# Gate/up weights of a hybrid decoder layer: the low parts of half of the weights by an accumulating DMA, and four Winograd pairs instead of two in seven blocks

## The chip, the core and the metric

One core of a Trainium2 chip runs the whole layer in one launch. The metric is the device time of that launch in microseconds (us), taken by the chip. The kernel before was timed three times: 1114.35, 1113.87 and 1112.45 us, median 1113.87 us. A fourth execution was profiled; its own time is 1112.63 us, and the span from its first to its last instruction is 1110.9 us.

## What is computed

One decoder layer on 256 tokens of width 2048, in fp32. A combined projection feeds a gated linear recurrence and a chunked retention, their outputs go through an output projection into the residual stream, and a SwiGLU feed-forward block follows. The change touches the feed-forward block only:

```
u  = rmsnorm(h, ln2_w)
ff = silu(u @ w_ffn_gate) * (u @ w_ffn_up)      # 256 x 2048 @ 2048 x 5632, twice
h  = h + ff @ w_ffn_down                        # 256 x 5632 @ 5632 x 2048
out = rmsnorm(h, final_norm_w)
```

The result must have fp32 accuracy, while TensorE is fed with a shorter format (fp32r). So each operand is cut into a high part, which is the operand cast to fp32r, and a low part, operand minus high part, and a product is made of three matmuls: high times high, high times low, low times high.

## The kernel before

**Blocks, pairs, halves.** Gate and up weights are walked in 11 blocks of 512 columns (`ffn_block`, block 0 to 10). A block has 8 steps, and a step takes 256 rows of the weights. Such a piece is called a pair here (class `Quad`): four weight tiles of 128 x 512, b11 and b12 (gate and up of the first 128 rows), then b22 and b21 (up and gate of the second 128 rows). It is loaded as two halves of 128 x 1024, 512 KB each, into tiles `raw`. The two token halves of u make the left operands a11, a12, a21, a22 (class `Left`, 128 x 128 each, made once and used by all 11 blocks).

**Eight products or seven.** An ordinary pair takes the eight products of the list `EIGHT`: each of the four results c11, c21, c12, c22 gets two. A *summed* pair (steps in `SUMMED`) follows Winograd's form of Strassen's scheme and takes seven products (list `SEVEN`) from sums t1 to t4 of the weights and s1 to s4 of the left operands. The results are gathered in PSUM over all 8 steps: four banks c11 to c22 (pool `aux`, 4 banks) and, for summed pairs, p1, p5, p6, p7 (pool `bank`, 4 banks). A product is three matmuls with 512 columns (L658, L659, L660).

**Who does what.** SyncE (SP) issues the loads of `raw` (L605). ScalarE (ACT) casts: tile `wh` (128 x 1024) is the high part (L101). VectorE (DVE) subtracts: tile `wl` is the low part (L102). In a summed pair DVE also makes t1 to t4 (L619, L620, L622, L623) into two more tiles of the pool of `raw` (named `sum`), which are cut like weights; b11 alone goes to `bh` and `bl` (128 x 512). GpSimd (POOL) does nothing in this stage. After the last step `ffn_post` adds results (L720, L722), applies the gate (L696 to L698), and `turn` transposes them on TensorE (L705) into `ff`.

**Buffers.** `raw` and `sum` share 5 buffers, `wh` has 4, `wl` has 4, and everything of 128 x 512 (pool `acts`) 58. A load of `raw` can go out only when the buffer it gets has been read for the last time; a cast into `wh` only when PE has used that buffer for the last time.

**Order.** Each engine works through its own queue strictly in order, and waits at the head of the queue. The order in the queues is not the order of the code: a scheduler orders instructions when the kernel is built, by priority and by what it holds to be ready. So PE's queue of one step mixes products of neighbouring steps: matmuls that need only a high part come first.

Of the kernel before, what the change touches and what calls it, by code (L numbers as in the profile page):

```python
# [14 lines left out]
P = 128  # L15
# [13 lines left out]

SUMMED = (2, 4)
SUMMED_DOWN = (2, 6, 10, 14, 18)


# [1 line left out]
def tile_hymba_layer(ctx: ExitStack, tc: tile.TileContext, A: dict, out: bass.AP):  # L37
# [181 lines left out]
    def defer(steps, f):  # L219
        later.append([steps, f])  # L220
# [321 lines left out]
    def out_post(f, ps):  # L542
        x = xs(f)
        if f < KT - 2:
            t = act_tile("op")[:, :S]
            halves(ps, t)
            v.tensor_tensor(out=x, in0=x, in1=t, op=ALU.add)
        else:
            v.tensor_tensor(out=x, in0=ps[:, :S], in1=x, op=ALU.add)
        if f % 2 == 0:  # L550
            hf[0] = act_tile("hf")
        act.activation(out=hf[0][:, (f % 2) * S : (f % 2) * S + S], in_=x, func=AF.Copy, scale=col(C_LN2 + f))
        if f % 2:
            hh[f // 2] = Left(hf[0], f // 2 in SUMMED)
        sq = sumsq[:, :S] if f == 0 else act_tile("sq")[:, :S]
        act.activation(out=sq, in_=x, func=AF.Square)
        if f:
            v.tensor_tensor(out=sumsq[:, :S], in0=sumsq[:, :S], in1=sq, op=ALU.add)
# [30 lines left out]
    class Quad:  # L589

        def __init__(self, src, sums, before=None):
            self.src, self.sums, self.before = src, sums, before
            self.parts = {}

        def cut(self, names, raw):
            h, l = (wpool.tile([P, 1024], F32R, tag=g, name=nm(g)) for g in ("wh", "wl"))
# [4 lines left out]
        def load(self, half):  # L603
            r = rpool.tile([P, 1024], F32, tag="raw", name=nm("raw"))
            nc.sync.dma_start(out=r, in_=self.src[:, half * 1024 : half * 1024 + 1024])  # L605
            if half == 0 and self.before:
                self.before()
            if not self.sums:
                self.cut(("b22", "b21") if half else ("b11", "b12"), r)
                return  # L610
            if half == 0:
                self.ra = r
                self.parts["b11"] = act_tile("bh", F32R), act_tile("bl", F32R)
                split(*self.parts["b11"], r[:, :512])
                return
            b11, b12, b22, b21 = self.ra[:, :512], self.ra[:, 512:], r[:, :512], r[:, 512:]
            ta, tb = (rpool.tile([P, 1024], F32, tag="raw", name=nm("sum")) for _ in range(2))
            t1, t2, t3, t4 = ta[:, :512], ta[:, 512:], tb[:, :512], tb[:, 512:]
            v.tensor_tensor(out=t1, in0=b11, in1=b12, op=ALU.add)  # L619
            v.tensor_tensor(out=t2, in0=t1, in1=b22, op=ALU.add)  # L620
            self.cut(("t1", "t2"), ta)
            v.tensor_tensor(out=t3, in0=b12, in1=b22, op=ALU.add)  # L622
            v.tensor_tensor(out=t4, in0=t2, in1=b21, op=ALU.add)  # L623
            self.cut(("t3", "t4"), tb)
            self.cut(("b22", "b21"), r)

    EIGHT = (
        ("c11", "a11", "b11"), ("c11", "a12", "b21"), ("c21", "a21", "b11"), ("c21", "a22", "b21"),
        ("c12", "a11", "b12"), ("c12", "a12", "b22"), ("c22", "a21", "b12"), ("c22", "a22", "b22"),
    )  # L630
    SEVEN = (
        ("p1", "a11", "b11"), ("p5", "s1", "t1"), ("p6", "s2", "t2"), ("p7", "s3", "t3"),
# [40 lines left out]

    def ffn_block(j):
        def after(i):
            if j == 0 and i == SUMMED[-1] + 1:
                norm2()
            if j in (1, 2) and i < 2:
                resid_tok(2 * j - 2 + i)
            if j == NB - 1 and i == 0:  # L680
                load_fw()

        ps = {}
        quads = [Quad(A["w_gu"][j * (KT // 2) + i], i in SUMMED) for i in range(KT // 2)]
        block(quads, hh, ffn_post(j, ps), ps, after=after)

    def ffn_post(j, ps):
# [21 lines left out]
        def post(c):  # L709
            if c == "p1":  # L710
                part["c11"] = act_tile("c11")
                act.copy(out=part["c11"], in_=ps[c])
            elif c == "p7":
                n = act_tile("n")
                v.tensor_tensor(out=n, in0=ps["p6"], in1=part["c11"], op=ALU.subtract)
                other("c12", "c12", n, ps["p5"])
                other("c21", "c21", n, ps["p7"])
                other("c22", "c22", part["c21"], ps["p5"])
            elif c in ("c11", "c12", "c22"):
                v.tensor_tensor(out=part[c], in0=ps[c], in1=part[c], op=ALU.add)  # L720
            elif c == "c21":
                v.tensor_tensor(out=part[c], in0=ps[c], in1=part[c], op=ALU.subtract)  # L722
            if c == "c12":
                gated(0)
            if c == "c22":
                gated(1)
                defer(2, lambda: turn(0))
                defer(3, lambda: turn(1))

        return post  # L730

# [316 lines left out]
```

## Time and profile before

| | |
|---|---|
| three runs | 1112.45 to 1114.35 us, median 1113.87 us |
| profiled execution | 1112.63 us, span 1110.9 us, 1.73 us outside the span |
| granted TensorE clock | 0.996 |
| gate/up blocks | from about 392 to about 868 us, 43.1 us each in the middle |
| down projection | from there to about 1096 us |

In the profile, "busy" is the time in which an engine executes; a wait is idle time that ended when another engine or a transfer released it. Lines of the profile name an instruction by its source line, its engine and its tiles (out<-in). PE is TensorE, PEld its weight load.

### The profile page before, as it was taken

The page shows a single profiled execution, that of the slowest core. Times are in us where ns is not written, and L with a number is a line of the kernel's source. Part 1 is how long each engine was busy: PE and PEld are TensorE (multiplying, and loading weights), DVE is VectorE, ACT ScalarE, POOL GpSimd, SP SyncE. Part 2 cuts the span into 40 slices and gives each one's busy share as a digit, 9 for nine tenths or more (in the row PEclk, how much of TensorE's full clock was granted, in tenths as well). Part 3 has the DMA queues.
Part 4 walks back from the last instruction along what each step waited for, and adds up shares of the span by engine and source line. Part 5 has one row for each costly group of instructions (what it writes and reads, how often), then busy time and mean ns, then how long its engine had stood idle before and what let it go on. Part 6 is the DMA issues. An engine that isn't in the chain of part 4 may idle for free.

```text
span 1110.9 us, 15099 instructions
## 1 busy us (share of the span) xinstructions
PE 1096.1 (99%) x5584; PEld 934.2 (84%) x5584; DVE 878.0 (79%) x1229; ACT 617.3 (56%) x826; POOL 58.1 (5%) x64
## 2 busy tenths in 40 slices
PE   9999999999999999999999999999999999999995
PEld 7998888889988988888888888888888888888884
DVE  7797799978766787788778877877887988886665
ACT  7666644468465665554554555545546665554453
POOL 0602230000000000000000000000000000020001
PEclk9999999999999999999999999999999999999998
DMA  9764575554665555645746646656556456655662
GB/s 329 236 198 151 174 252 167 169 188 146 201 198 187 171 192 183 212 147 186 239 138 219 226 152 227 193 186 228 170 187 229 171 176 198 233 186 193 192 220 80
DMA packets 62218, 214.74 MB, mean 193 GB/s; under 512 B 7105, under 2 KB 7489, under 8 KB 62145
## 3 DMA queue, kind: packets, MB, share of 16 engines
q1 hardware_dynamic: 61344, 211.70, 57.8%
q0 software_dynamic: 512, 1.57, 0.4%
q8 instruction: 43, 0.70, 0.3%
q10 hardware_dynamic: 288, 0.52, 0.1%
q14 instruction: 31, 0.25, 0.1%
HBM read 211.67 MB, written 2.10 MB: 192 GB/s over the span
## 4 chain that ended last, share of the span: by engine, by line
PE 97%; ACT 1%; POOL 1%; DVE 0%; DMA 0%; issue 0%; SPq 0%; DVEq 0%; POOLq 0%
PE c L658 18%; PE c L659 18%; PE c L660 18%; PE fm L140 10%; PE fm L141 5%; PE fm L146 3%; PE fm L147 3%; PE fm L145 3%; PE p L660 3%; PE p L658 3%; PE p L659 3%; PE tm L156 3%; PE tm L157 3%; PE tm L158 3%; PE ft L705 1%; POOL sumsq L289 1%
## 5 line engine op out<-in xcount | busy, mean ns | idle before, releaser
L102 DVE TENSOR_TENSOR wl<-raw,wh 128x1024 fp32r<-128x1024 f32 (+1 forms) x368 | 440.7, 1209 | 151.2 <-ACT wh L101 149.4
L101 ACT CAST wh<-raw 128x1024 fp32r<-128x1024 f32 (+1 forms) x368 | 375.8, 1032 | 297.3 <-PE c L660 145.1
L659 PE MATMUL c<-wl,ah 128*128 128x512 f32 x864 | 333.1, 391 | 0.0
L660 PE MATMUL c<-wh,al 128*128 128x512 f32 x864 | 331.8, 389 | 0.0
L658 PE MATMUL c<-wh,ah 128*128 128x512 f32 x864 | 292.1, 389 | 0.0
L659 PEld LDWEIGHTS c<-wl,ah 128*128 128x128 f32 x864 | 162.2, 188 | 33.5 <-DVE wl L102 0.4
L658 PEld LDWEIGHTS c<-wh,ah 128*128 128x128 f32 x864 | 162.1, 188 | 33.4
L660 PEld LDWEIGHTS c<-wh,al 128*128 128x128 f32 x864 | 162.3, 188 | 33.0
L101 ACT CAST wh<-sum 128x1024 fp32r<-128x1024 f32 x64 | 66.8, 1054 | 81.3 <-PE c L660 52.7
L140 PE MATMUL fm<-u,wh 128*128 128x512 f32 x256 | 90.7, 398 | 0.0
L140 PE MATMUL fm<-y,wh 128*128 128x512 f32 x224 | 78.9, 398 | 0.0
L102 DVE TENSOR_TENSOR wl<-sum,wh 128x1024 fp32r<-128x1024 f32 x64 | 76.7, 1217 | 2.2 <-ACT wh L101 1.6
L146 PE MATMUL fm<-u,wh 128*128 128x256 f32 x256 | 72.7, 284 | 0.0
L145 PE MATMUL fm<-u,wh 128*128 128x256 f32 x256 | 72.7, 284 | 0.0
L147 PE MATMUL fm<-u,wl 128*128 128x256 f32 x256 | 72.3, 283 | 0.0
L141 PE MATMUL fm<-u,wl 128*128 128x256 f32 x256 | 71.9, 281 | 0.0
L141 PE MATMUL fm<-y,wl 128*128 128x256 f32 x224 | 62.4, 281 | 0.0
L807 POOL TENSOR_TENSOR htok<-htok,fw 128x512 f32<-128x512 f32 (+1 forms) x7 | 10.5, 1509 | 914.0 <-ACT junk L805 914.0
L140 PEld LDWEIGHTS fm<-u,wh 128*128 128x128 f32 x256 | 48.1, 188 | 11.7
L619 DVE TENSOR_TENSOR sum<-raw 128x512 f32<-128x512 f32 x32 | 22.0, 687 | 37.9 <-DMA raw<-in_w_down 23.0
L140 PEld LDWEIGHTS fm<-y,wh 128*128 128x128 f32 x224 | 41.9, 188 | 10.2
L146 PEld LDWEIGHTS fm<-u,wh 128*128 128x128 f32 x256 | 49.1, 192 | 0.1
(242 smaller groups left out, 1489.5 us busy)
## 6 DMA issues: line engine op xcount, KB each, us to landing
raw<-in_w_gu SPq DMA_DIRECT2D x176, 512.0 KB, 5.0
raw<-in_w_down SPq DMA_DIRECT2D x88, 512.0 KB, 5.1
raw<-in_w_out SPq DMA_DIRECT2D x32, 512.0 KB, 4.2
raw<-in_w_lx SPq DMA_DIRECT2D x16, 512.0 KB, 4.9
raw<-in_w_k SPq DMA_DIRECT2D x16, 512.0 KB, 3.7
raw<-in_w_q SPq DMA_DIRECT2D x16, 512.0 KB, 4.2
raw<-in_w_rg SPq DMA_DIRECT2D x16, 512.0 KB, 3.7
raw<-in_w_lg SPq DMA_DIRECT2D x16, 512.0 KB, 3.8
```

What stands on the lines that cost most here:

```text
L101: act.copy(out=dst_h, in_=src)
L102: v.tensor_tensor(out=dst_l, in0=src, in1=dst_h.bitcast(F32), op=ALU.subtract)
L140: pe.matmul(ps, wh, hl, start=first, stop=False)
L141: pe.matmul(ps[:, :S], wl, hl[:, :S], start=False, stop=last)
L145: pe.matmul(ps, wh, hl[:, :S], start=first, stop=False)
L146: pe.matmul(ps, wh, hl[:, S:], start=False, stop=False)
L147: pe.matmul(ps, wl, hl[:, :S], start=False, stop=last)
L156: pe.matmul(ps, ah, wh, start=first, stop=False)
L157: pe.matmul(ps, ah, wl, start=False, stop=False)
L658: pe.matmul(p, ah, bh, start=firsts[c] == m, stop=False)
L659: pe.matmul(p, ah, bl, start=False, stop=False)
L660: pe.matmul(p, al, bh, start=False, stop=last)
```

## The change

Seven blocks (`N_ADDED`, block 0 to 6) treat the second half of each pair (b22, b21) in a new way, `cut_added`: ACT casts the high part as before; ACT then writes minus the high part into two tiles `ln` of 128 x 512 (from the pool `acts`); and GpSimd issues for each of them a DMA of 256 KB, from SBUF to SBUF, that adds the raw weights to what stands there. The result is the low part that DVE's subtraction made before. That is 16 such DMAs a block, 112 in all.

In these blocks four pairs are summed (steps 1, 3, 4, 6) in place of two (2, 4); blocks 7 to 10 keep 2 and 4. Left operands are summed for the five steps of both lists. A summed pair cuts its second half before its sums, not after. `EIGHT` is in another order, for all blocks: the four products with b11 and b12 come first. `norm2` runs after step 6 of block 0 (after step 5 before), and both transposing steps of `turn` run after the first step of the next block (the second one a step later before).

```
-SUMMED = (2, 4)
+SUMMED = (1, 3, 4, 6)
+SUMMED_LATE = (2, 4)
+N_ADDED = 7
...
-            hh[f // 2] = Left(hf[0], f // 2 in SUMMED)
+            hh[f // 2] = Left(hf[0], f // 2 in SUMMED + SUMMED_LATE)
...
+        def cut_added(self, names, raw):
+            h = wpool.tile([P, 1024], F32R, tag="wh", name=nm("wh"))
+            act.copy(out=h, in_=raw)
+            for n, name in enumerate(names):
+                hn, l = h[:, n * 512 : n * 512 + 512], act_tile("ln", F32R)
+                act.activation(out=l, in_=hn.bitcast(F32), func=AF.Copy, scale=-1.0)
+                pool.dma_start(out=l.bitcast(F32), in_=raw[:, n * 512 : n * 512 + 512], accum_op=ALU.add)
+                self.parts[name] = hn, l
...
-                self.cut(("b22", "b21") if half else ("b11", "b12"), r)
+                (self.cut_added if half and self.added else self.cut)(("b22", "b21") if half else ("b11", "b12"), r)
...
             v.tensor_tensor(out=t2, in0=t1, in1=b22, op=ALU.add)
+            (self.cut_added if self.added else self.cut)(("b22", "b21"), r)
             self.cut(("t1", "t2"), ta)
...
             self.cut(("t3", "t4"), tb)
-            self.cut(("b22", "b21"), r)
...
-        ("c11", "a11", "b11"), ("c11", "a12", "b21"), ("c21", "a21", "b11"), ("c21", "a22", "b21"),
+        ("c11", "a11", "b11"), ("c21", "a21", "b11"), ("c12", "a11", "b12"), ("c22", "a21", "b12"),
...
-            if j == 0 and i == SUMMED[-1] + 1:
+            if j == 0 and i == SUMMED[-1]:
                 norm2()
...
-        quads = [Quad(A["w_gu"][j * (KT // 2) + i], i in SUMMED) for i in range(KT // 2)]
+        added = j < N_ADDED
+        sums = SUMMED if added else SUMMED_LATE
+        quads = [Quad(A["w_gu"][j * (KT // 2) + i], i in sums, added=added) for i in range(KT // 2)]
...
-                defer(3, lambda: turn(1))
+                defer(2, lambda: turn(1))
```

The scheduler orders the queues anew. Two places matter for the prediction. In the rows below a number behind a name only tells tiles apart, and line numbers of the changed kernel are larger than those of the profile.

**Place 1, the border between two blocks.** PE's queue before, up to the first matmul into the next block's c11 (here c11_1204; the block that ends has c12_1127 and c22_1128):

```order
L658 MATMUL c12_1127_5849<-wh_1185_6095,ah_785_4339 128x512
L659 MATMUL c12_1127_5849<-wl_1186_6096,ah_785_4339 128x512
L660 MATMUL c12_1127_5849<-wh_1185_6095,al_786_4340 128x512
L658 MATMUL c22_1128_5856<-wh_1182_6065,ah_785_4339 128x512
L659 MATMUL c22_1128_5856<-wl_1183_6066,ah_785_4339 128x512
L660 MATMUL c22_1128_5856<-wh_1182_6065,al_786_4340 128x512
L658 MATMUL c22_1128_5856<-wh_1185_6095,ah_785_4339 128x512
L659 MATMUL c22_1128_5856<-wl_1186_6096,ah_785_4339 128x512
L660 MATMUL c22_1128_5856<-wh_1185_6095,al_786_4340 128x512
L658 MATMUL c11_1204_6189<-wh_1188_6101,ah_634_3518 128x512
```

The new c11 gets the bank of the old c11, whose last matmul stands 17 rows ahead of it. PE's queue now, at the border between blocks 4 and 5 (old results c11_1222, c12_1224, c22_1225, new c11_1321), from the last matmul that uses wh_1277:

```order
L673 MATMUL c11_1222_6100<-wh_1277_6331,al_773_4221 128x512
L671 MATMUL c11_1222_6100<-wh_1285_6351,ah_795_4370 128x512
L672 MATMUL c11_1222_6100<-wl_1286_6352,ah_795_4370 128x512
L673 MATMUL c11_1222_6100<-wh_1285_6351,al_796_4371 128x512
L671 MATMUL c11_1222_6100<-wh_1288_6381,ah_795_4370 128x512
L672 MATMUL c12_1224_6108<-ln_1289_6383,ah_795_4370 128x512
L673 MATMUL c12_1224_6108<-wh_1288_6381,al_796_4371 128x512
L672 MATMUL c22_1225_6112<-ln_1289_6383,ah_795_4370 128x512
L673 MATMUL c22_1225_6112<-wh_1288_6381,al_796_4371 128x512
L671 MATMUL c11_1321_6508<-wh_1292_6391,ah_634_3518 128x512
```

The first row into the new c11 stands 3 rows behind the last one into the old c12, whose bank it gets: it waits until DVE has added the old c12 up. It stands 9 rows behind the last use of wh_1277. At the borders between the first seven blocks it is 3 rows everywhere, behind block 6 it is 7, and at the four borders after that 10.

DVE's queue before, at its border (wl_1192 is the last split of weights ahead of it, L720 and L722 add results up):

```order
L102 TENSOR_TENSOR wl_1192_6132<-raw_1190_6129,wh_1191_6131 128x1024
L720 TENSOR_TENSOR c11_1173_6029<-c11_1125_5835,c11_1173_6029 128x512
L722 TENSOR_TENSOR c21_1176_6044<-c21_1126_5842,c21_1176_6044 128x512
L619 TENSOR_TENSOR sum_1211_6226<-raw_1201_6183 128x512
L720 TENSOR_TENSOR c12_1175_6042<-c12_1127_5849,c12_1175_6042 128x512
```

DVE's queue now:

```order
L105 TENSOR_TENSOR wl_1293_6392<-raw_1291_6389,wh_1292_6391 128x1024
L707 TENSOR_TENSOR c22_1298_6415<-c21_1297_6413,p5_1238_6162 128x512
L632 TENSOR_TENSOR sum_1309_6480<-raw_1303_6436 128x512
L105 TENSOR_TENSOR bl_1305_6439<-raw_1303_6436,bh_1304_6438 128x512
L735 TENSOR_TENSOR c12_1296_6411<-c12_1224_6108,c12_1296_6411 128x512
L735 TENSOR_TENSOR c22_1298_6415<-c22_1225_6112,c22_1298_6415 128x512
```

The addition of the old c12 stands behind bl_1305, the low part of the next block's b11, which needs bh_1304 from ACT. So it is at the borders 3 to 4, 4 to 5 and 5 to 6; at the three borders before them only a row like sum_1309 stands ahead. ACT's queue before, there:

```order
L101 CAST wh_1188_6101<-raw_1187_6099 128x1024
L101 CAST wh_1191_6131<-raw_1190_6129 128x1024
L696 ACTIVATE th_1196_6162<-c11_1173_6029,r2_half_119 128x512
L696 ACTIVATE th_1197_6173<-c21_1176_6044,r2_half_119 128x512
L101 CAST bh_1202_6185<-raw_1201_6183 128x512
L101 CAST wh_1194_6137<-raw_1193_6135 128x1024
```

ACT's queue now:

```order
L104 CAST wh_1292_6391<-raw_1291_6389 128x1024
L603 CAST wh_1300_6428<-raw_1299_6426 128x1024
L606 ACTIVATE ln_1301_6430<-wh_1300_6428 128x512
L606 ACTIVATE ln_1302_6433<-wh_1300_6428 128x512
L104 CAST bh_1304_6438<-raw_1303_6436 128x512
L603 CAST wh_1311_6484<-raw_1308_6478 128x1024
```

The cast into bh_1304 now stands behind the cast into wh_1300, which gets the buffer of wh_1277, and behind both negations.

**Place 2, the second half of an ordinary pair between two summed ones.** Before, that is step 3, between the summed pairs 2 and 4. ACT's queue before; wh_1225 is the high part of that half, wh_1237 that of t1 and t2 of pair 4:

```order
L101 CAST wh_1220_6246<-raw_1219_6244 128x1024
L707 COPY ff_1223_6279<-ft_1222_6274 128x512
L101 CAST bh_1228_6289<-raw_1227_6287 128x512
L101 CAST wh_1225_6283<-raw_1224_6281 128x1024
L101 CAST wh_1237_6324<-sum_1235_6320 128x1024
```

Now it is step 2, between the summed pairs 1 and 3. ACT's queue now; wh_1231 is the high part of that half, ln_1232 and ln_1233 its negations, wh_1244 the high part of the second half of pair 3:

```order
L603 CAST wh_1231_6144<-raw_1230_6142 128x1024
L603 CAST wh_1244_6189<-raw_1241_6183 128x1024
L606 ACTIVATE ln_1232_6146<-wh_1231_6144 128x512
L606 ACTIVATE ln_1233_6149<-wh_1231_6144 128x512
L104 CAST bh_1235_6154<-raw_1234_6152 128x512
```

The negations stand behind a cast that needs another load, raw_1241; that load gets its buffer when DVE has cut t3 and t4 of pair 1. The buffer of wh_1231 is that of pair 1's second half, last used 25 rows of PE's queue ahead of the first use of ln_1232. Before, no negation exists, and DVE's subtraction follows a cast in its own queue.

More of the change, by code (lines that the diff above doesn't have):

```diff
@@ L589, in tile_hymba_layer, with __init__ @@
     class Quad:
-        def __init__(self, src, sums, before=None):
-            self.src, self.sums, self.before = src, sums, before
+        def __init__(self, src, sums, before=None, added=False):
+            self.src, self.sums, self.before, self.added = src, sums, before, added
             self.parts = {}
+        def cut_added(self, names, raw):
[6 more added lines that the diff above has]
+                self.parts[name] = hn, l
         def cut(self, names, raw):
@@ L624, in load @@
             self.cut(("t3", "t4"), tb)
-            self.cut(("b22", "b21"), r)
     EIGHT = (
-        ("c11", "a11", "b11"), ("c11", "a12", "b21"), ("c21", "a21", "b11"), ("c21", "a22", "b21"),
-        ("c12", "a11", "b12"), ("c12", "a12", "b22"), ("c22", "a21", "b12"), ("c22", "a22", "b22"),
+        ("c11", "a11", "b11"), ("c21", "a21", "b11"), ("c12", "a11", "b12"), ("c22", "a21", "b12"),
+        ("c11", "a12", "b21"), ("c21", "a22", "b21"), ("c12", "a12", "b22"), ("c22", "a22", "b22"),
     )
```

## The prediction

> **What bounds the kernel now.** I read the page's busy times and chain first, then the waits of PE, then the gate/up stage by windows.
>
> ```profile
> PE 1096.1 (99%) x5584; PEld 934.2 (84%) x5584; DVE 878.0 (79%) x1229; ACT 617.3 (56%) x826; POOL 58.1 (5%) x64
> PE 97%; ACT 1%; POOL 1%; DVE 0%; DMA 0%; issue 0%; SPq 0%; DVEq 0%; POOLq 0%
> PE warm L94 <- DVE eps_t L87: 1.0, 1, 1.0
> PE tm L156 <- ACT u L277: 0.8, 2, 0.5
> PE rms L250 <- POOL sumsq L290: 0.7, 1, 0.7
> 580.00:640.00 60.00, 60.00 (x270) 49.62 (x269) 49.65 (x57) 32.27 (x35) 0.00 (x0) 1.00 0.65 214
> ```
>
> PE is 97% of the chain that ended last, and the only three waits of PE (rows three to five: total, times, longest) are on lines ahead of the gate/up blocks. In the window of 60 us from the gate/up blocks (PE, PEld, DVE, ACT, POOL, clock, DMA share, GB/s) PE is always busy at full clock, DVE 83%, ACT 54%. So a matmul less is time gained at PE's pace, and any wait that PE gets is time lost in full. The pace is read from the chain in order of time, where L658 rows recur block by block:
>
> ```profile
> 535.56 0.91 PE c L658 x4
> 578.68 0.91 PE c L658 x4
> 621.81 0.91 PE c L658 x4
> ```
>
> Four matmuls take 0.91 us, 0.2275 each; a block takes 43.1 us. Its 62 products of three matmuls make 42.3 us, and its 8 transposes have the remaining 0.8, about 0.10 each.
>
> **The change part by part.** *Products.* Two more summed pairs in each of seven blocks: 14 products, 42 matmuls, less. 42 x 0.2275 = **-9.6 us**, all on the path. This is certain if nothing else waits.
>
> *Work of DVE and ACT.* Rows of the gate/up stage:
>
> ```profile
> L102 DVE TENSOR_TENSOR wl<-raw,wh 128x1024 fp32r<-128x1024 f32 x121 | 145.5, 1220 | 60.2 <-ACT wh L101 60.0
> L622 DVE TENSOR_TENSOR sum<-raw,raw 128x512 f32<-128x512 f32 x18 | 12.3, 682 | 0.0
> L102 DVE TENSOR_TENSOR bl<-raw,bh 128x512 fp32r<-128x512 f32 x17 | 11.6, 681 | 0.0
> L101 ACT CAST wh<-raw 128x1024 fp32r<-128x1024 f32 x120 | 124.6, 1053 | 97.1 <-PE c L660 85.8 <-DMA raw<-in_w_gu 8.6 <-PE p L660 1.7
> L101 ACT CAST bh<-raw 128x512 fp32r<-128x512 f32 x17 | 10.4, 614 | 2.0 <-DMA raw<-in_w_gu 1.9
> L696 ACT ACTIVATE th<-c,r_half 128x512 f32<-128x512 f32 x16 | 10.7, 716 | 16.6 <-DVE c L720 16.6
> ```
>
> DVE loses 8 subtractions a block (8 x 1.22 = 9.8 us). Each of the two new summed pairs gives it four sums (2.7), two splits of sums (2.44) and a half split in place of a whole one (-0.54): 4.6, together 9.3. DVE stays where it was. ACT gets 16 negations a block. None is in the trace; the cast of 512 columns took 0.614, the tanh 0.716, and back to back copies of 512 start 0.51 apart (below). I take 0.6: 9.6 us, and 1.05 + 0.61 for each new summed pair, 12.9 in all. ACT goes from 54% of 43.1 = 23.2 us to 36 of 41.8. It still fits; the cost is in the order of its queue.
>
> *Borders of blocks (place 1).* The steps of the chain, from the trace:
>
> ```profile
> 585.55 0.39 PE L660 MATMUL c<-wh,al 128*128 128x512 f32 x1
> 585.98 1.05 ACT L101 CAST wh<-raw 128x1024 fp32r<-128x1024 f32 x1 [1.68 <-PE c L660]
> 587.06 1.23 DVE L102 TENSOR_TENSOR wl<-raw,wh 128x1024 fp32r<-128x1024 f32 x1 [0.80 <-ACT wh L101]
> 579.84 0.68 DVE L102 TENSOR_TENSOR bl<-raw,bh 128x512 fp32r<-128x512 f32 x1
> 580.44 0.68 DVE L622 TENSOR_TENSOR sum<-raw,raw 128x512 f32<-128x512 f32 x1
> 660.76 0.59 ACT L707 COPY ff<-ft 128x512 f32<-128x512 f32 x1 [0.82 <-PE ft L705]
> 661.27 1.05 ACT L101 CAST wh<-raw 128x1024 fp32r<-128x1024 f32 x1
> ```
>
> An engine released by a matmul starts 0.43 after that matmul's start (585.55 to 585.98), DVE starts 0.03 after a cast ends, and two DVE operations of 512 start 0.60 apart. At three borders the queues now make one chain: last use of wh_1277, 0.43, cast into wh_1300 1.05, two negations 1.2, cast bh 0.61, 0.03, bl 0.60, the sum of old c12 0.68, and only then the first matmul of the new block: 4.60 us. PE has 9 rows of work there, 2.05 us. It waits 2.55 (2.4 to 2.8 with negations of 0.51 to 0.72): 3 x 2.55 = 7.7. At the three borders before, only the sum of c12 lies between: 0.43 + 0.68 against 3 rows, 0.68: 0.43 each, 1.3. **+8.9 us.** Before, 17 rows (3.9 us) stood there. Behind block 6 there are 7 to 10 rows, 1.6 to 2.3 us, against 1.11: nothing, unless DVE hangs on a load ahead of the sum.
>
> *The accumulating DMA (place 2).* Its time to landing is not in the trace. The nearest rows, us from issue to landing: the eight decay tables of 192 KB that GpSimd loads from HBM (minimum, median, maximum; the first alone; its issue in ns), and the first stores of 256 KB at the end, from SP, with quiet queues; then the loads of `raw` in the feed-forward block, and of w_k:
>
> ```profile
> DMA to landing us min/median/max: 3.5/5.9/6.2
> DMA to landing us min/median/max: 3.5/3.5/3.5
> L414 POOL DMA_DIRECT2D decay<-in_decay x8: 536/536/732, 142.7 to 146.6; - x8
> DMA to landing us min/median/max: 2.2/2.6/2.6
> DMA to landing us min/median/max: 3.1/5.0/7.8
> raw<-in_w_k SPq DMA_DIRECT2D x16, 512.0 KB, 3.7
> ```
>
> So 2.2 to 6.2; I take 3.3, near the first decay table: same queue, similar size, loads beside it, but no HBM. PE's queue allows less. From the matmul that frees the buffer for t3 and t4 of pair 1 to the first use of ln_1232 there are 52 rows, 8 of them transposes: 44 x 0.2275 + 0.8 = 10.8 us. In them lie 0.43, the cast 1.05, DVE's split 1.25, the load that this releases (5.0), the cast of wh_1244 1.05 and the negation 0.66: 9.4. That leaves 1.4 for the DMA. If the load takes 3.7, PE's release of wh_1231's own buffer counts: 25 rows, 5.7 us, less 0.43, two casts (2.1) and 0.66, leaves 2.5. A landing of 3.3 makes PE wait 0.8 to 1.9; I take 1.3: 7 x 1.3 = **+9.1 us**. The other six second halves of a block have 4.4 us or more, or, at the border, what the wait there gives them.
>
> [...]
>
> *Without a price.* The Left operands get three more sums, at most 3 x 4 us of DVE while the output projection runs (380 to 400: DVE 16.2 of 20):
>
> ```profile
> 380.00:400.00 20.00, 20.00 (x117) 17.75 (x116) 16.21 (x24) 13.52 (x21) 0.00 (x0) 1.00 0.46 159
> ```
>
> They are used a step or more later, which hides them; uncovered, up to 3 us. The moved `norm2` and `turn` have 15 rows and more of PE ahead of their first user: 0. The 112 issues on POOL, 0.54 each, meet an idle engine.
>
> **The sum.** 1110.9 - 9.6 + 8.9 + 9.1 = 1119.3, and 1.7 outside the span: 1121. The profiled execution (1112.63) lies 1.2 below the median of the runs, so **1122 us** for the median, 0.7% slower. Three runs spread by 0.17%, so under 0.2% is no change.
>
> **The rivals.** *R1, faster:* a wait at a border is short, since ACT's casts run ahead of PE, and the DMA lands within 2.5. Only the short border waits stay (6 x 0.43 = 2.6): 1112.6 - 9.6 + 2.6 = 1105.6, with half of the rest up to 1110. For it: ACT waits for PE's buffers often now, PE for ACT never. Against it: the chain at the border holds by order and durations alone. It decides when PE's waits stay under 1.1 us a block. Chance 0.27.
>
> *R2, the DMA engines become the bound.*
>
> ```profile
> q1 hardware_dynamic: 61344, 211.70, 57.8%
> q0 software_dynamic: 512, 1.57, 0.4%
> ```
>
> 211.7 MB in 57.8% of 1110.9 us is 330 GB/s at full share. The second row is GpSimd's queue, a share of the same 16 engines. A block loads 8.4 MB (25.4 us) and now adds 4.2 MB. Counted once that is 12.7 us, 38 of 41.8: tight, with longer loads. If an addition costs a read of both sides, 25.4: 50.8 us a block, 7.7 more than 43.1, 1112.6 + 7 x 7.7 = 1166. [...] No row shows what an addition costs. Half of the excess gives about 1140. Chance 0.15.
>
> *R3, no change:* PE's waits come to 1.1 to 1.7 us a block, against the 1.37 that its six matmuls save: 1110.4 to 1114.9. Chance 0.13.
>
> That the change doesn't do what it says is no case: the queues hold 112 additions and 42 matmuls less.
>
> **How the numbers follow.** My forecast (1115 to 1135) has 0.45. Faster 0.27, same 0.13, slower 0.45 + 0.15 = 0.60. The range reaches from 1104, which takes in most of R1, to 1146, which leaves out the upper half of R2. The forecast's own range is 1115 to 1135, from a DMA landing of 2.5 to 4.5.
>
> **What would show it.** Right: PE waits at six borders for DVE's L735 (three times some 2.5 us) and once a block for a DMA into ln; ACT near 85% in blocks 0 to 6; 43.5 to 46 us per block there, 43.1 in blocks 7 to 10. Wrong: PE without waits in blocks 0 to 6 and 41.8 us a block (R1), or a DMA share near 1 and loads of 7 us and more (R2).

## The result, and the profile after

The changed kernel took 1246.39 us (median of four runs, 1240.65 to 1252.62) against 1113.16 us of the kernel before on the same chip (four runs, 1112.21 to 1114.35): a ratio of 1.120, interval 1.116 to 1.124. It is 12% slower; the prediction had 0.7%, with 1146 us as its upper end. The profiled execution took 1252.62 us, its span 1250.8 us.

First the page after: busy times, then the chain that ended last.

```profile
PE 1135.8 (91%) x5542; PEld 939.1 (75%) x5542; DVE 887.2 (71%) x1272; ACT 699.6 (56%) x969; POOL 156.9 (13%) x176
PE 62%; DMA 20%; issue 11%; ACT 3%; DVE 2%; POOL 1%; SPq 0%; POOLq 0%; DVEq 0%; ACTq 0%
```

PE has lost the 42 matmuls (5584 to 5542), yet its share of the chain fell from 97% to 62%, and transfers have 20% where they had none (10% additions, 9% loads of `raw`). Where that is, the windows of 60 us show (PE, PEld, DVE, ACT, POOL, clock, DMA share, GB/s): three from blocks 0 to 6, and one from the late blocks.

```profile
460.00:520.00 60.00, 48.03 (x199) 35.92 (x198) 34.25 (x44) 36.17 (x51) 14.14 (x16) 0.94 0.80 203
580.00:640.00 60.00, 46.03 (x185) 33.96 (x184) 34.81 (x46) 33.82 (x46) 14.12 (x16) 0.96 0.84 212
700.00:760.00 60.00, 46.97 (x185) 35.46 (x185) 32.41 (x42) 33.91 (x45) 14.14 (x16) 0.94 0.77 197
940.00:1000.00 60.00, 60.00 (x270) 49.70 (x269) 47.23 (x54) 31.64 (x36) 0.00 (x0) 1.00 0.66 221
```

The late blocks, which have no additions, are as fast as ever. In the first seven PE is idle for 12 to 14 us of 60 in the windows shown (11 to 15 in all), and what it does is slower too. Put down to these seven, the difference of the spans is (1250.8 - 1110.9) / 7 = 20.0 us on top of 43.1, 63.1 us a block. PE's waits, over the whole run (total, times, longest), and the additions themselves, issue in ns and landing in us:

```profile
PE c L672 <- DMA ln<-raw: 73.5, 50, 4.9
PE c L671 <- ACT wh L104: 8.8, 8, 1.7
PE c L671 <- DVE c L735: 5.7, 5, 2.4
```

```profile
L607 POOL DMA_DIRECT2D ln<-raw x112: 860/906/1467, 398.1 to 818.6; - x112
DMA to landing us min/median/max: 3.3/6.5/11.9
```

The wait for the additions is there, but 50 times and not 7. The loads of `raw` have kept their median of 5.0 us over all blocks (5.4 between 400 and 810 us). These three kinds of wait come to 88 us, all of PE's waits in the stage to 96. To explain are the 139.9 us between the spans and the 9.6 that the 42 matmuls should have saved, 149.5 us. Most of the rest is PE's pace: its busy time is 49 us more than 1096.1 - 9.6. Here is a stretch behind a wait of 2.87 us (start, duration, the wait in brackets):

```profile
619.21 0.80 PE L672 MATMUL c<-ln,sh 128*128 128x512 f32 x1 [2.87 <-DMA ln<-raw]
619.80 0.63 PE L673 MATMUL c<-wh,sl 128*128 128x512 f32 x1
620.23 0.63 PE L671 MATMUL c<-wh,ah 128*128 128x512 f32 x1
620.65 0.63 PE L672 MATMUL c<-wl,ah 128*128 128x512 f32 x1
621.08 0.63 PE L673 MATMUL c<-wh,al 128*128 128x512 f32 x1
621.51 0.63 PE L672 MATMUL c<-wl,ah 128*128 128x512 f32 x1
621.93 0.47 PE L673 MATMUL c<-wh,al 128*128 128x512 f32 x1
...
622.48 0.39 PE L673 MATMUL c<-wh,al 128*128 128x512 f32 x1
```

The matmuls behind this wait start 0.43 us apart, not 0.23. Eight intervals from 619.21 to 622.48 take 3.27 us in place of 8 x 0.2275 = 1.82: the wait costs 1.45 us beyond its own length. The granted clock shows why (windows as above; in so short a window the DMA share can read above 1):

```profile
615.27:618.68 3.41, 1.07 (x5) 0.55 (x3) 0.99 (x2) 2.73 (x4) 1.49 (x2) 1.00 1.06 237
618.68:622.10 3.42, 2.89 (x7) 2.32 (x8) 1.49 (x3) 0.57 (x1) 0.28 (x1) 0.50 1.08 247
```

The clock was granted at one half (0.50) from 618.68 to 622.10. In this trace every stretch at half clock in the stage lasts 3.41 us or twice that, 58 us in all, and in the 3.41 us ahead of each PE had been idle for 51% to 97% of the time. Two short waits can add up to that (ahead of 639.16 they were 0.77 us and 0.96 us of a longer one), and one alone need not: a wait of 1.54 us that ended at 614.68 was followed by matmuls at full pace.

### The profile page after: what moved, and what is told of

Its sections match the earlier page's. It is cut to its first block, busy times and chain, and to the rows that moved or that the text cites. A ratio compares the mean times of both kernels' runs of the same rounds, so it can differ in the third digit from the quotient of the medians.

```text
span 1250.8 us, 15600 instructions
## 1 busy us (share of the span) xinstructions
PE 1135.8 (91%) x5542; PEld 939.1 (75%) x5542; DVE 887.2 (71%) x1272; ACT 699.6 (56%) x969; POOL 156.9 (13%) x176
## 3 DMA queue, kind: packets, MB, share of 16 engines
q1 hardware_dynamic: 61344, 211.70, 50.8%
q0 software_dynamic: 16640, 30.94, 13.7%
## 4 chain that ended last, share of the span: by engine, by line
PE 62%; DMA 20%; issue 11%; ACT 3%; DVE 2%; POOL 1%; SPq 0%; POOLq 0%; DVEq 0%; ACTq 0%
DMA ln<-raw 10%; PE c L672 10%; PE c L673 10%; PE c L671 10%; DMA raw<-in_w_gu 9%; PE fm L143 9%; PE fm L144 4%; PE tm L159 2%; PE tm L161 2%; PE tm L160 2%; PE fm L149 2%; PE fm L150 2%; PE fm L148 2%; PE p L671 1%; PE p L672 1%
## 5 line engine op out<-in xcount | busy, mean ns | idle before, releaser
L104 ACT CAST wh<-raw 128x1024 fp32r<-128x1024 f32 (+1 forms) x298 | 304.3, 1027 | 265.9 <-PE c L673 96.6
L105 DVE TENSOR_TENSOR wl<-raw,wh 128x1024 fp32r<-128x1024 f32 (+1 forms) x298 | 358.9, 1211 | 106.9 <-ACT wh L104 105.6
L671 PE MATMUL c<-wh,ah 128*128 128x512 f32 (+1 forms) x780 | 274.6, 401 | 15.1 <-ACT wh L104 8.8
L672 PE MATMUL c<-wl,ah 128*128 128x512 f32 (+1 forms) x640 | 255.0, 399 | 0.0
L607 POOL DMA_DIRECT2D ln<-raw x112 | 99.0, 1046 | 542.1 <-ACT ln L606 224.2
L105 DVE TENSOR_TENSOR wl<-sum,wh 128x1024 fp32r<-128x1024 f32 x92 | 111.0, 1221 | 46.6 <-ACT wh L104 45.7
L672 PEld LDWEIGHTS c<-wl,ah 128*128 128x128 f32 x640 | 123.9, 194 | 26.1
L603 ACT CAST wh<-raw 128x1024 fp32r<-128x1024 f32 x56 | 58.4, 1050 | 95.3 <-DMA raw<-in_w_gu 52.7
L672 PE MATMUL c<-ln,ah 128*128 128x512 f32 x140 | 60.3, 431 | 27.3 <-DMA ln<-raw 27.1
L606 ACT ACTIVATE ln<-wh 128x512 fp32r<-128x512 f32 x112 | 64.2, 621 | 0.7
```

Of the source, the lines that this page charges most:

```text
L104: act.copy(out=dst_h, in_=src)
L105: v.tensor_tensor(out=dst_l, in0=src, in1=dst_h.bitcast(F32), op=ALU.subtract)
L606: act.activation(out=l, in_=hn.bitcast(F32), func=AF.Copy, scale=-1.0)
L607: pool.dma_start(out=l.bitcast(F32), in_=raw[:, n * 512 : n * 512 + 512], accum_op=ALU.add)
L671: pe.matmul(p, ah, bh, start=firsts[c] == m, stop=False)
L672: pe.matmul(p, ah, bl, start=False, stop=False)
```

## The experiments

Three theories stood against each other. *DMA engines*: the additions use up the time of the 16 engines. *Hold*: an addition reads its raw buffer until it lands, so the ring of five buffers runs dry and loads go out late. *Read*: PE waits for each landing, since the cutting runs too little ahead. A fourth, *order*, needs no addition at all: the borders, the queues, four pairs in place of two.

| what runs | us, median | ratio to before, interval |
|---|---|---|
| after | 1246.4 | 1.120 (1.116 to 1.124) |
| new order alone | 1115.0 | 1.0016 (1.0007 to 1.0026) |
| additions, two pairs | 1205.6 | 1.083 (1.081 to 1.085) |
| four pairs, no additions, nothing in their place | 1134.4 | 1.020 (1.019 to 1.022) |
| four pairs, low parts by DVE | 1146.8 | 1.030 (1.029 to 1.032) |
| additions as traffic only | 1174.6 | 1.055 (1.054 to 1.057) |
| traffic and hold, no read | 1225.7 | 1.101 (1.099 to 1.103) |
| traffic and read, no hold | 1221.9 | 1.099 (1.096 to 1.103) |
| plain copies | 1179.8 | 1.060 (1.057 to 1.062) |

**The order alone.**

```
-SUMMED = (1, 3, 4, 6)
+SUMMED = (2, 4)
-N_ADDED = 7
+N_ADDED = 0
```

> The changed kernel without its additions and without its two new summed pairs in any block: only the new order of the eight products, the new place of the split of b22 and b21 in a summed pair, the earlier second norm and the earlier transposes are left. Theory of the raw ring (the additions hold the five raw buffers, so that loads start late) and theory of the DMA engines (the additions take the engines' time): both need the additions, so 1113 us, within 3. Theory of the borders (the short border between blocks, three rows of PE in place of 17, is where time goes by itself): 1 to 9 us above the kernel before, 1114 to 1122 us, with waits of PE for DVE L735.

1115.02 us, 2.0 above before on the same chip, in the ranges of both answers. In the middle of the stage PE waited three times for L735, 1.0 us together. A short border by itself costs next to nothing. (With this list `norm2` runs after step 4, in this run and the next, and not after step 6.)

**The additions without the new pairs.**

```
-SUMMED = (1, 3, 4, 6)
+SUMMED = (2, 4)
```

> The changed kernel with its 112 additions, but with two summed pairs per block as before, so the 42 matmuls are back. Raw ring: 20 buffers of the ring are used per block in place of 24, so the loss shrinks, but stays: about 55 us a block, 1195 us (1170 to 1225). DMA engines: the same traffic in the same blocks, so the same block time as in the changed kernel, about 62 us, 1245 us (1235 to 1255). Direct wait (PE waits for each addition's own landing, whatever the ring does): 16 additions a block as before, 1230 to 1250 us. If neither, and it is the two new summed pairs that bring the loss: 1113 us.

1205.64 us, 56.0 us a block by its span of 1201.4. It lies in the range of the raw ring (the five buffers of `raw`), but the DMA share was 0.85 to 0.92, higher than in the changed kernel, so this run tells nothing apart alone. It does show that the additions cost 91 us (1205.6 - 1115.0) without the new pairs.

**No additions, and nothing in their place.**

```
-                pool.dma_start(out=l.bitcast(F32), in_=raw[...], accum_op=ALU.add)
-                self.parts[name] = hn, l
+                self.parts[name] = hn, hn
```

> The changed kernel with its four summed pairs, its order and its negations, but without any addition; TensorE reads the high part in place of their result, so the low parts of the second halves are left out. It is the base for the runs with the additions (hold, traffic, read). If these three are the whole loss: 42 matmuls less are worth 9.6 us, so 1104 to 1108 us, and up to 1114 if the borders of blocks cost what the prediction had for them (8.9 us, three waits of some 2.5 us for DVE). If the loss lies in the summed pairs and the work of ACT: over 1125 us.

1134.44 us, the last of the cases named. So the additions are worth 112 us of the loss (1246.4 - 1134.4), and something else costs more than the 42 matmuls save: the kernel before (1112.2 beside this run) less 9.6 would be 1102.6, and this is 32 above. The trace shows a place: PE's largest wait in the stage is the seven waits for DVE's sums of an old block. First that row, then PE and DVE at one border, then what the late load waited for (from the chain that ended last):

```profile
PE c L670 <- DVE c L734: 15.5, 7, 3.4
```

```profile
570.91 0.39 PE L672 MATMUL c<-wh,al 128*128 128x512 f32 x1
574.41 0.47 PE L670 MATMUL c<-wh,ah 128*128 128x512 f32 x1 [3.11 <-DVE c L734]
...
575.61 0.63 PE L671 MATMUL c<-wh,ah 128*128 128x512 f32 x1
576.04 0.63 PE L672 MATMUL c<-wh,al 128*128 128x512 f32 x1
```

```profile
562.34 1.22 DVE L105 TENSOR_TENSOR wl<-raw,wh 128x1024 fp32r<-128x1024 f32 x1
568.24 0.69 DVE L631 TENSOR_TENSOR sum<-raw 128x512 f32<-128x512 f32 x1 [4.68 <-DMA raw<-in_w_gu]
...
571.19 0.68 DVE L729 TENSOR_TENSOR n<-p,c 128x512 f32<-128x512 f32 x1
571.79 0.68 DVE L636 TENSOR_TENSOR sum<-sum,raw 128x512 f32<-128x512 f32 x1
572.39 1.27 DVE L706 TENSOR_TENSOR c<-n,p 128x512 f32<-128x512 f32 x2
573.59 1.28 DVE L734 TENSOR_TENSOR c<-c,c 128x512 f32<-128x512 f32 x2
```

```profile
561.20 1.24 DVE wl L105
562.46 5.66 DMA raw<-in_w_gu
```

DVE stands for 4.68 us at the first sum of a summed pair, whose load is late: it went out only when DVE had made the low part of a tile of sums, which shares the ring with `raw`. The old block's last sums are queued behind it, and PE needs them to free a bank. PE stands for 3.1 us and soon after starts matmuls 0.43 us apart (575.61 and 576.04). All of PE's waits in the stage come to 19.0 us. The granted clock was 0.97 in three of the five windows of 60 us from 460 to 760 us and 1.00 in the other two, an estimate of 11 us at half clock (3 x 60 x 0.03 x 2).

**Four pairs, low parts by DVE.**

```
-        quads = [Quad(A["w_gu"][j * (KT // 2) + i], i in sums, added=added) for i in range(KT // 2)]
+        quads = [Quad(A["w_gu"][j * (KT // 2) + i], i in sums) for i in range(KT // 2)]
```

> The changed kernel with all of its products right, but the low parts of the second halves by DVE as before: four summed pairs without additions. DVE has 34.2 us a block before (0.79 of 43.1) and 4.6 more for each new pair, 43.4 against PE's 41.8. Traffic, hold and read as the whole loss: DVE is then the bound, 43.5 to 45.5 us a block, 1113 to 1130 us. If summed pairs cost by their order or by the ring of raw buffers (24 tiles a block in place of 20): over 1140 us.

1146.77 us, the second answer: the pairs cost by themselves. PE waited 19.5 us for L735 at six borders, where DVE is later still; DVE was busy for 52 to 55 us of 60, so its work may have a part in it.

**Traffic alone; traffic and hold; traffic and read.** The first has both edits below, the second only that of `parts`, the third only that of the source (`konst` is a tile of ones):

```
-                pool.dma_start(out=l.bitcast(F32), in_=raw[...], accum_op=ALU.add)
+                pool.dma_start(out=l.bitcast(F32), in_=konst, accum_op=ALU.add)
-                self.parts[name] = hn, l
+                self.parts[name] = hn, hn
```

> The changed kernel with its 112 additions as pure traffic: they read a constant tile, and TensorE reads the high part in place of their result, so they hold no raw buffer and nobody on TensorE's path waits for them; left out is the low part of the second halves. DMA engines: 49 us of engine time a block at a share near 0.95 gives some 52 us a block, 1165 to 1180 us. Raw ring and direct wait: the whole loss goes, 41.8 to 43 us a block, 1103 to 1115 us, loads at their 5 us.

> The changed kernel with all additions made from the raw weights, but TensorE reads the high part where it read their result, so nothing on its path waits for a landing by itself; what is left out is the low part of the second halves in the products. What is left is the hold of the raw buffers and the load on the DMA engines, which by shares and block times need some 49 us a block (0.83 of 60 us, before 0.575 of 43.1). DMA engines: the engines set the pace, 50 to 56 us a block, 1165 to 1205 us. Raw ring: the hold of the buffers alone, 1165 to 1225 us. Direct wait: the loss goes, 1105 to 1120 us.

> The changed kernel, but the additions read a constant tile in place of the raw weights, so that a raw buffer is free after the cast; what is left out are the low parts of the second halves (they come out as a constant minus the high part). Traffic of the DMA engines, issues on POOL, and PE's wait for each addition are kept. Raw ring: the loss goes, 42 to 45 us a block, 1105 to 1125 us. DMA engines: unchanged, 1240 us (1230 to 1255), with a DMA share of 0.8 or more. Direct wait: PE still waits for the landings, 1190 to 1250 us.

1174.59, 1225.68 and 1221.87 us: in the range named for the engines, just above that of the raw ring, and in that of the direct wait. Traffic that nobody waits for costs 40 us over the run without it (1134.4). Its windows show why (DMA share is the last but one column; the windows ahead of these and behind have 0.91 and 0.88):

```profile
520.00:580.00 60.00, 52.51 (x228) 41.85 (x227) 38.48 (x49) 39.03 (x52) 15.26 (x19) 0.97 0.97 247
580.00:640.00 60.00, 54.47 (x228) 41.92 (x227) 41.27 (x52) 40.88 (x54) 16.78 (x19) 0.97 0.99 252
640.00:700.00 60.00, 49.52 (x210) 38.10 (x210) 40.03 (x53) 40.12 (x54) 17.67 (x20) 0.98 0.99 255
```

The engines are full here. Before, they needed 0.575 x 43.1 = 25 us a block; in the changed kernel 0.8 x 63.1 = 50. That makes, as an estimate, a floor of some 50 us a block, whoever waits. On this floor the hold adds 51 us and the read 47; both together add 72, not 98. That they delay the same next tile would explain it, but no run shows it. The waits of the two runs show the paths: with the hold, SP's queue stands for an addition to let a raw buffer go, and PE waits for casts that come late; with the read, PE waits for the landings.

```profile
SPq L618 <- DMA ln<-raw: 169.0, 34, 8.3
ACT wh L603 <- DMA raw<-in_w_gu: 79.3, 45, 7.2
PE c L671 <- ACT wh L104: 21.0, 15, 3.3
PE c L671 <- ACT wh L603: 20.2, 17, 6.2
```

```profile
PE c L674 <- DMA ln<-konst: 74.3, 44, 5.0
```

The constant tile as a source hardly moved the landing here: 6.7 us in the median with the read, 6.5 in the changed kernel. No theory is right alone. Traffic has its price by itself; hold and read have theirs on top of it, about half of it (24.5 and 20.7 us) where the other one is there already.

**Plain copies.**

```
-                pool.dma_start(out=l.bitcast(F32), in_=raw[...], accum_op=ALU.add)
+                pool.dma_start(out=l.bitcast(F32), in_=raw[...])
```

> The changed kernel, but the 112 transfers copy the raw weights and add nothing (the low parts of the second halves come out as the whole weights, so the sum on top of minus the high part is left out). Same issues, same buffers, same waits. DMA engines: if adding costs a second read, a copy takes the engines half of 1.5 us; they then need about 38 us a block, and the time falls to 1120 to 1170 us. Direct wait and raw ring: the time follows the landing alone; if it falls from a median of 6.5 to 4.5 us, 1170 to 1200 us, if it stays, 1235 to 1255 us.

1179.81 us, in the range named for a landing of 4.5 us, and 67 less than the changed kernel, from one attribute. GpSimd's queue in this run (packets, MB, share) and its transfers, then the queue of the changed kernel:

```profile
q0 software_dynamic: 9472, 30.94, 6.8%
```

```profile
L607 POOL DMA_DIRECT2D ln<-raw x112: 538/538/584, 397.7 to 751.4; - x112
DMA to landing us min/median/max: 2.3/4.6/7.5
```

```profile
q0 software_dynamic: 16640, 30.94, 13.7%
```

The same 30.94 MB. Without the decay tables (512 packets, 0.4% of 1110.9 us) a copy of 256 KB takes 80 packets and (0.068 x 1177.9 - 4.4) / 112 = 0.68 us of all engines, an addition 144 packets and (0.137 x 1250.8 - 4.4) / 112 = 1.49 us. The engines were busy at 0.67 to 0.74 with the copies and not the bound; yet 1180 is still 45 above the run without any transfer. We put that to the hold and the read, with a landing of 4.6; copies as traffic alone were not run.

**Half of the additions, and what holds them.** b22 goes to DVE:

```
+                if n == 0:
+                    v.tensor_tensor(out=l, in0=raw[:, :512], in1=hn.bitcast(F32), op=ALU.subtract)
+                    self.parts[name] = hn, l
+                    continue
```

> The changed kernel with only the second half (b21) of each second tile made by an addition, the first (b22) by a subtraction of DVE: 56 additions, eight a block. DVE has 41 to 42 us of work a block. DMA engines: 37 us a block, no longer the bound, 42 to 45 us a block, 1110 to 1130 us. Direct wait and raw ring: each second tile still waits for one landing, and its buffer is held as long, so well over half of the loss stays: 1170 to 1225 us.

1203.31 us (ratio 1.082, 1.080 to 1.083), in the second range. The engines stand at 0.66 to 0.70, and 56 us over the same kernel by DVE (1146.8) stay. PE's wait in the stage:

```profile
PE c L676 <- DMA ln<-raw: 46.4, 30, 2.8
```

Three runs looked for the reason: the same from `konst`; the same with t1 to t4 in three buffers of their own; and the same with the high parts of the second tiles in three buffers of their own, beside the four of `wh`.

```
-                pool.dma_start(out=l.bitcast(F32), in_=raw[...], accum_op=ALU.add)
+                pool.dma_start(out=l.bitcast(F32), in_=konst, accum_op=ALU.add)
```

```
-            ta, tb = (rpool.tile([P, 1024], F32, tag="raw", name=nm("sum")) for _ in range(2))
+            ta, tb = (own[0].tile([P, 1024], F32, tag="sum", name=nm("sum")) if self.added else ...
```

```
-            h = wpool.tile([P, 1024], F32R, tag="wh", name=nm("wh"))
+            room, tag = (own[0], "who") if own else (wpool, "wh")
+            h = room.tile([P, 1024], F32R, tag=tag, name=nm("wh"))
```

> Half of the additions (b21 alone; 1203 us with the raw weights as their source), but from a constant tile, so they hold no raw buffer; left out is the low part of b21. DMA share stays near 0.69, so the engines aren't the bound. The same kernel without any addition, all by DVE, took 1147 us. Hold as the cause of the 56 us between: 1147 to 1165 us. TensorE's own wait for the landing as the cause: 1185 to 1205 us.

> Half of the additions (b21 alone, b22 by DVE) and the tiles of sums in three buffers of their own, everything computed. Half of the additions alone gave 1203 us with a DMA share of 0.69, so the engines are not its bound. Hold of the raw buffers as its cause: 1115 to 1165 us. Wait of TensorE for the landing, with too few tiles of weights cut ahead, as its cause: 1175 to 1205 us.

> Half of the additions (1203 us, everything computed), but the high parts of the second tiles in blocks 0 to 6 have three buffers of their own, so seven tiles of high parts in place of four, and a cast can run further ahead of TensorE. Wait for the landing with too few tiles cut ahead as the cause: well under 1203, 1150 to 1185 us, with fewer waits of ACT for PE. If loads and raw buffers hold it anyway: 1195 to 1210 us.

1202.26, 1203.21 and 1195.26 us (1.081, 1.083, 1.074): twice in the range of the wait, and in the third run in that of loads and raw buffers. The first doesn't settle the hold, for the raw buffer is still held, now by DVE's subtraction of b22. SP waited 173.4 us for additions in the run with half of them; here it waits as long for that subtraction:

```profile
SPq L624 <- DVE ln L609: 169.7, 41, 13.2
```

Besides, from the constant tile the landing took 6.5 us and not 4.5. The sums' buffers decide nothing here, and more room for high parts gives back 8 us. There ACT's longest row of waits for PE's buffers falls from 31.6 to 7.3 us, its waits for loads rise from 103 to 130, and SP still waits 178 us for additions: with one ring widened the next one binds. How the 56 us divide between these stays open; a run with half of the additions that PE doesn't read was not made.

**All additions, sums in buffers of their own.** 16 tiles a block in the ring of five, not 24, by the edit of `ta, tb` above.

> The changed kernel with all of its work, but in blocks 0 to 6 the tiles of sums (t1 to t4) come from three buffers of their own, so the ring of five raw buffers serves 16 tiles a block in place of 24. Raw ring: most of the loss goes; by 40 us of buffer time less per block over five buffers, about 8 us a block or more: 1105 to 1190 us, and the loads start without SP waiting for DVE's sums. DMA engines: 1235 to 1255 us, or slower, since more is in flight. Direct wait: 1200 to 1250 us.

1224.18 us, 22 less: in the range of the direct wait, and what the sums' tiles cost in the ring is the smaller part. With eight buffers SP waits more for additions, not less, 261.6 us in all and 119.5 in the changed kernel:

```profile
SPq L619 <- DMA ln<-raw: 261.6, 54, 9.7
```

**What four pairs cost without additions.** Three runs changed the run of 1134.4 us: the old list `EIGHT`; the pairs 2, 4, 5, 6; the sums in their own buffers (the edit of `ta, tb` above).

```
-        ("c11", "a11", "b11"), ("c21", "a21", "b11"), ("c12", "a11", "b12"), ("c22", "a21", "b12"),
+        ("c11", "a11", "b11"), ("c11", "a12", "b21"), ("c21", "a21", "b11"), ("c21", "a22", "b21"),
...
```

```
-SUMMED = (1, 3, 4, 6)
+SUMMED = (2, 4, 5, 6)
```

> The run without additions (four summed pairs 1, 3, 4, 6, low parts of the second halves left out, 1134 us) with the eight products of an unsummed pair in the order of the kernel before: 17 rows of PE, 3.9 us, at the border of blocks in place of 3. Theory of the border (sums of the old block hang in DVE's queue behind the first sum of pair 1, which waits for its load, and PE stands 3.1 us and then runs at half pace): the border covers most of it, 1103 to 1112 us. Theory that four pairs cost by the ring of raw buffers, wherever PE stands: 1125 to 1137 us.

> The run without additions (1134 us) with the new order kept, but the four summed pairs at 2, 4, 5, 6, so that pair 1 has no sums that wait in DVE's queue ahead of the old block's. If sums of pair 1 at the border are the cause: 1103 to 1112 us, and no wait of PE for DVE over 1 us at the borders. If the short border by itself: as the run without additions, 1128 to 1137 us. If four pairs cost by the ring: 1125 to 1140 us, with waits inside the block.

> The run without additions (four summed pairs, 1134 us, low parts of the second halves left out) with the tiles of sums in three buffers of their own, so the ring of five raw buffers serves 16 tiles a block in place of 24. Ring of raw buffers as the cause of what four pairs cost: 1103 to 1115 us. Border of the blocks and the order of DVE's and ACT's queues as the cause: 1127 to 1137 us.

1134.37, 1131.83 and 1141.24 us (ratios 1.018, 1.017, 1.025). None takes the loss away: not the long border, not moving pair 1, not the sums' own buffers. The first two lie where the ring was named as the cause, but with the ring relieved the third is slower still, above both of its ranges. PE still waited for DVE's last sums, 9.2 us in four waits, 12.9 in five and 10.3 in six. The place is shown, and at one border what held the load; what makes four pairs slow as a whole isn't settled.

**Can more pairs be had in another way?** The kernel before with pairs 2, 4, 6 in all blocks; and the same with GpSimd's own subtraction for the last 512 columns of each second tile, in the down projection too.

```
-SUMMED = (2, 4)
+SUMMED = (2, 4, 6)
...
+            pool.tensor_tensor(out=l[:, 512:], in0=raw[:, 512:], in1=h[:, 512:].bitcast(F32), op=ALU.subtract)
```

> The kernel before with three summed pairs (2, 4, 6) in each of the eleven blocks, no additions, the old order: 33 matmuls less, 7.5 us, and 38.8 us of DVE against 42.4 of PE per block. If DVE's queue hides it: 1105 to 1108 us, faster than both kernels. If DVE at 0.92 makes PE wait by as much: 1111 to 1120 us.

> The kernel before with three summed pairs (2, 4, 6) in all blocks (1132 us, DVE at 0.86), where GpSimd subtracts the last 512 columns of each second tile, in the feed-forward and the down blocks, and DVE the first 512: nothing goes through the DMA engines, and DVE loses 4.3 us a block. GpSimd's products of 128x512 take 1.7 us, 13.8 us a block. If DVE's queue was what made three pairs slow: 1104 to 1110 us, faster than both kernels. If the 0.5 us later low part or the ring of buffers makes PE wait: 1113 to 1135 us.

1132.01 us (1.018, 1.016 to 1.019) and 1193.61 us (1.072, 1.069 to 1.074), both above every range named. Three pairs lose with no transfer added, and why isn't shown. With GpSimd it is worse, and DVE's rows are longer (first with GpSimd beside it, then the run with three pairs; the mean in ns stands behind the comma):

```profile
L600 DVE TENSOR_TENSOR wl<-raw,wh 128x512 fp32r<-128x512 f32 x63 | 72.4, 1149 | 1.7 <-ACT wh L599 1.5
L102 DVE TENSOR_TENSOR wl<-raw,wh 128x1024 fp32r<-128x1024 f32 x40 | 60.1, 1501 | 2.8 <-ACT wh L101 2.7
```

```profile
L102 DVE TENSOR_TENSOR wl<-raw,wh 128x1024 fp32r<-128x1024 f32 x116 | 139.3, 1218 | 9.1 <-ACT wh L101 9.1
```

A subtraction of 512 columns took 1.15 us in place of the 0.68 of such rows before, and a whole one 1.50 us in place of 1.22: half a subtraction in the run with GpSimd cost DVE about as much as the whole one in the run without it. What makes DVE slower there isn't shown. No version that beats the kernel before was found.

## Why the prediction was wrong

**The bound** was read rightly: PE waits for nothing before, so every wait is lost time. Too kindly, though: a wait was priced at its length, and where the clock falls to half PE loses more behind it (1.45 us behind the wait of 2.87). Nor need PE be idle throughout the time ahead of such a stretch: here it was idle for 1.73 us of 3.41, by a wait of 0.77 us and the first part of one of 1.38, and 3.41 us at half clock followed, with matmuls 0.43 us apart and not 0.23.

```profile
635.75:639.16 3.41, 1.68 (x7) 0.73 (x5) 1.71 (x3) 2.33 (x4) 1.77 (x2) 1.00 1.09 281
639.16:642.58 3.42, 3.00 (x7) 2.45 (x8) 2.74 (x6) 1.04 (x1) 0.00 (x0) 0.50 0.82 143
```

```profile
639.58 0.77 PE L671 MATMUL c<-wh,ah 128*128 128x512 f32 x1 [1.38 <-DVE c L735]
640.15 0.63 PE L672 MATMUL c<-wl,ah 128*128 128x512 f32 x1
640.57 0.63 PE L673 MATMUL c<-wh,al 128*128 128x512 f32 x1
```

**Products, DVE, ACT.** 42 matmuls went, as counted. ACT gained 82 us (617.3 to 699.6; predicted 7 x 12.9 = 90), a negation took 0.62 us (taken 0.6), and DVE moved by 9 us, all told. The work was sized rightly.

**The borders (8.9 us).** The mechanism, PE waiting for DVE's last sums, was right. In the changed kernel these waits came to 5.7 us, five of them; without the additions to 15.5, seven of them. The prediction allowed for "unless DVE hangs on a load ahead of the sum" only behind block 6; the border shown above, between earlier blocks, is such a case. The sum without the DMA's term would have been 1112.2 - 9.6 + 8.9 = 1111.5 us; the run without additions took 1134.4. So in place of 8.9, four pairs cost 32 us beyond the saved matmuls: 19.0 of it in PE's waits and, from the estimate of 11 us at half clock, some 5 in slower matmuls.

**The accumulating DMA (9.1 us): the step that failed.** It set the landing to 3.3 us, "near the first decay table", and let PE wait once a block, since "the other six second halves of a block have 4.4 us or more". 3.3 is the minimum of what came; the median was 6.5, above 4.4 and above the upper end of 6.2. PE waited 50 times, 73.5 us, at 38 of the 56 second halves (counted by the order of their issue). At the half of step 2, the one that the term was about, that is 15.0 us. The other 58.5 are at halves that got no price, 46.4 of it in summed pairs:

```profile
L672 PE MATMUL c<-ln,sh 128*128 128x512 f32 x28 | 15.2, 542 | 46.4 <-DMA ln<-raw 46.4
```

The median of the eight decay tables, 5.9, stood in the same quoted row and was nearer: the first table had only loads of `raw` beside it (DMA share 0.73), the later ones their fellows too (0.87 to 0.89), as additions have. Nor does the term name the raw buffer that an addition holds, nor SP's queue behind it. It measured 112 us (1246.4 - 1134.4).

**R2, the engines (chance 0.15).** Its arithmetic was the best part of the text: 25.4 us a block if an addition reads both sides, 50.8 together, 1166 us. Measured: 50 us of engine time a block, and 1174.6 us with traffic alone. The wrong step was to set it beside the waits as a rival: both hold at once, traffic with 40 us alone and hold and read with 72 on top. R1 and R3 fell with the first window: 63 us a block, not 41.8.

**What would show it.** Named as the sign of R2 were a share near 1 and loads of 7 us. Neither is in the changed kernel (0.77 to 0.84, 5.0 us). It took the run with traffic alone to see the share at 0.97 to 0.99, with loads of 6.2 us in the median between 400 and 820 us. ACT was at 56% and not 85%, with the work as predicted (36): 0.56 x 63.1 = 35 us a block.

## What to carry to other kernels

A transfer in place of an engine's operation was paid three times here: in the time of the DMA engines, in the buffer that it reads until it lands, and in the reader's wait (40, 51 and 47 us, 112 together). Price all three, take their sum as the upper end, since they overlap, and take the landing from transfers in the same company, by their median. Where an engine has no waits before, ask how many microseconds of work are cut ahead of it, and compare that with the new latency. And a freed engine is worth nothing by itself: here more pairs lost time in every form tried.

## What the hardware showed

- An addition of 256 KB from SBUF to SBUF took 0.91 us to issue, 144 packets, 1.49 us of all 16 engines and 6.5 us to land (3.3 to 11.9) at a DMA share of 0.77 to 0.84; a copy of the same took 0.54 us, 80 packets, 0.68 us and 4.6 us (2.3 to 7.5) at 0.67 to 0.74.
- In the gate/up blocks of the changed kernel the TensorE clock fell to half for 3.41 us, or twice that, each time after 3.41 us in which PE was idle for 51% or more; the emptiest such time, counted on in steps of 3.41 us, that was not followed by it had 56% (from 775.70 us). At half clock matmuls started 0.43 us apart, not 0.23: six of them behind the wait of 2.87 us and six behind that of 1.38.
- In the run where GpSimd subtracted the other 512 columns (1.66 us each), DVE's subtraction of 512 columns took 1.15 us, and 0.68 in the kernel before.
